# The recurrent mixer in another order: keys and queries of all heads first, values later, gates and u beside inverses and scans, levels and inverses in batches

## The chip, the cores and the metric

The kernel runs on one core of one Trainium2 chip. The number that counts is the device time of one execution in microseconds (us). Before the change it is 1601.41 us, the median of 3 runs (1600.74 to 1604.13). Engines are named as in the profile: PE is the matrix engine (PEld its weight loads), DVE the vector engine, ACT the scalar engine, POOL the general engine, SP the engine that issues the DMAs.

## What is computed

The reference is a block of two layers followed by a second block with sparse, dilated and cross attention. The change lies in the first mixer, which is run on 256 context tokens and 256 latent tokens together (512 columns here). It projects the normed input, and feeds two branches, a gated chunk mixer and a gated delta rule:

```
a_u, a_v, qkv, gate, alpha_raw, beta_raw = split(h @ w_in)
y_a = gelu(a_u) * (ws @ layer_norm(gelu(a_v)) + bs)      # chunks of 128 tokens, 4 groups
q, k, v = silu(dwconv3(qkv));  q, k = l2(q), l2(k)       # 4 heads of 128
T = inverse(I + strict_tril(beta k k^T * decay))         # per head, direction and chunk
S_t = a_t S_{t-1} (I - b_t k_t k_t^T) + b_t k_t v_t^T    # scan over chunks, forward and backward
o = rms_norm(o_forward + o_backward) * silu(gate)
y = concat(y_a, o) @ w_out
```

Everything is fp32 to the eye of the caller. A product of two matrices is made of three matmuls on rounded halves (hi and lo of the weight, hi and lo of the data), so one 1024 x 128 weight tile against 512 columns is 8 x 3 = 24 matmuls.

## The kernel before, in words

A tile framework schedules the program: the code is written stage by stage, pools give each tile name a number of buffers, and the framework lays all instructions out into one fixed order for each engine. An engine runs its list in order, so an instruction that waits holds back all that stands behind it. Parts under `high_priority` are put as early as their inputs allow. The pools of PSUM (the accumulators that PE writes) limit how many results can be in flight: `mm` for the wide products, `s1`, `lv`, `su` for the small ones of the recurrent branch.

Layer 0 before the change, with the time at which it runs in the trace:

- `gmlp` (to 51 us the a_v product, then to 74 us the a_u product, then the chunk mix with `wsT`, an elementwise product, 16 transposes and copies into `ya`).
- `gdn`: `stage1(h)` for heads 0 to 3. Each projects K, Q and V of one head (3 x 24 matmuls of 512 columns), evacuates with the three-tap convolution (line 751, DVE), transposes, makes the norms, the decay matrix `AT` and the strict triangle, which goes through memory to `blocks` (16 x 16 inverses by elimination, on DVE, 30 instructions for each direction on 64 partitions) and to `levels` (merging 16 to 32 to 64 to 128 by 32 x 32 and 64 x 64 matmuls). Parts of the modulation product (`ps_ad<-rawa`) are put between them by the list `GF`.
- `inverses(0)`, the four gate projections, then with new pools `inverses(2)` beside `scan(0)` (240 to 299 us). A scan carries four chains (two heads, two directions) through four steps; one step is up to five 128 x 128 matmuls into one `su` tile, with r (DVE, line 1255), vn (ACT, line 1258), the state S (DVE, line 1267) and o (line 1277 or ACT) between them. Three `su` tiles exist.
- `out("w_out0a", ...)` over the gmlp half (96 matmuls of 512 columns) beside `scan(1)`, then `out("w_out0b", ...)` twice: context columns beside the end of `scan(1)`, latent columns after it. Then the norm of the FFN and its first matmul, `ps_mm<-fh`, at 377 us.

In before the helper `mm` is line 366, the weight halves are made by ACT `whi` (line 344) and DVE `wlo` (line 345), a transpose is line 389. The DMA of a weight chunk is line 350, that of the modulation weights (`rawa`) line 640. In the changed file these lines are one lower.

Of the kernel before, what the change touches and what calls it, by code (L numbers as in the profile page):

```python
# [10 lines left out]
F32 = mybir.dt.float32  # L11
# [15 lines left out]
SWAP = ()  # L27
# [3 lines left out]
ROOT = ('pre', 'gmlp', 'gdn', 'ffn0', 'mla', 'ffn1', 'sparse')  # L31
# [10 lines left out]
GF = (6, 6, 4, 0, 0, 8)  # L42
SPS = (3, 3)
FILL = (12, 4)
AUN = 2
# [110 lines left out]
def _layout(x):  # L156
# [24 lines left out]
    vec["abs"] = x["a_bs"][0].T  # L181
# [21 lines left out]
    o["w_au"] = _tm(w[:, 0:512], 2)  # L203
# [4 lines left out]
    w = _fm(x["ab_w_out"][0]).reshape(4, 2, P, 2, 512).transpose(3, 0, 2, 1, 4).reshape(2, 4, P, 1024)  # L208
    o["w_out0a"], o["w_out0b"] = w[0], w[1]
# [53 lines left out]
class K:  # L263
# [127 lines left out]
    def rsqrt(self, v, n, scale=1.0, eps=EPS, plus=None):  # L391
# [4 lines left out]
        T = lambda dt=F32: self.small.tile([P, 16], dt, name=self.nm("rq"), tag="rq", bufs=12)[:, :n]  # L396
# [511 lines left out]
    def layer0(self):  # L908
        nc, d = self.nc, self.d
# [6 lines left out]
        yap = self.pool("ya")  # L916
        yp = yap.__enter__()
        ya = [yp.tile([P, 512], F32, name=f"ya{g}", tag=f"ya{g}", bufs=1) for g in range(4)]
        self.psum(mm=4, sm=2, ad=2)
        with self.pool("ring0") as self.ring, self.pool("aring0") as self.aring:  # L920
            self.RAW, self.HL, self.RAWA = 2, 2, 16
            gmp = self.pool("gm")
            gm = self.gmlp(gmp.__enter__(), hi, lo, ya)
# [19 lines left out]
            next(gm, 0)  # L943
            gmp.__exit__(None, None, None)
        self.phase("gdn")
        self.fillers = [f for j in range(4, 10) for f in self.ada4(0, j)]
        g1p = self.pool("gdn")
        g1 = g1p.__enter__()
        self.psum(mm=2, s1=3, lv=2, ad=1)
        g3p = self.pool("gdn3")  # L950
        g3 = g3p.__enter__()
        with self.pool("ring1") as self.ring, self.pool("gdn2") as g2:
            self.RAW, self.HL = 2, 2
            self.aring, self.RAWA = g2, 4
            inverses, scan = self.gdn(g1, g2, g3, hi, lo)
        hpool.__exit__(None, None, None)
        xp = self.ctx.enter_context(self.pool("xp", side="right"))
        self.x = xp.tile([P, 8, 512], F32, name="x", tag="x", bufs=1)
        ypool = self.pool("y0", side="right")
        yp2 = ypool.__enter__()  # L960
        self.outer(nr=1, ad=1, su=SPS[1])
        self.psum(lv=SPS[0])
        spool = self.pool("scan", side="right")
        scan = scan(spool.__enter__(), lambda h, s, o: self.split(o, yhi[:, 4 + h, s], ylo[:, 4 + h, s]))
        yhi = yp2.tile([P, 8, 512], F32R, name="yhi", tag="yhi", bufs=1)
        ylo = yp2.tile([P, 8, 512], F32R, name="ylo", tag="ylo", bufs=1)
        for k in range(4):
            self.split(ya[k], yhi[:, k], ylo[:, k])
        inverses(2)
        g3p.__exit__(None, None, None)  # L970
        with self.tc.high_priority():
            scan(0)
        for k in range(8):
            nc.sync.dma_start(self.x[:, k], d["x0"][:, k])
        self.psum(mm=SPS[0])

        def out(w, k0, a, b, tag="mm"):

            for j in range(4):
                wh, wl = [w.rearrange("p (i k m) -> p i k m", i=2, k=4) for w in self.chunk(d[w][j])]  # L980
                for i in range(2):
                    ps = self.ps(tag)
                    for k in range(4):
                        self.mm3(ps[:, :b - a], (wh[:, i, k], wl[:, i, k]), (yhi[:, k0 + k, a:b], ylo[:, k0 + k, a:b]),
                                 k == 0, k == 3)
                    for h, (u, v) in enumerate(halves):
                        if a <= u and v <= b:
                            xj = self.x[:, 2 * j + i, u:v]
                            nc.vector.scalar_tensor_tensor(xj, ps[:, u - a:v - a], m[:, 16 + 2 * j + i, 1 - h:2 - h], xj,
                                                           op0=ALU.mult, op1=ALU.add)  # L990
        yring = self.pool("yring")
        self.ring, self.RAW, self.HL = yring.__enter__(), 2, 3
# [16 lines left out]
    def gmlp(self, gp, hi, lo, ya):

        nc, d = self.nc, self.d
        lng = gp.tile([P, 512], F32, name="lng", tag="lng", bufs=1)
        lnb = gp.tile([P, 512], F32, name="lnb", tag="lnb", bufs=1)
        ws = gp.tile([P, 4, P], F32, name="wsT", tag="wsT", bufs=1)
        v = gp.tile([P, 4, 512], F32, name="gv", tag="gv", bufs=1)
        u = gp.tile([P, 4, 512], F32, name="gu", tag="gu", bufs=1)
        st = gp.tile([P, 4, 6], F32, name="gst", tag="gst", bufs=1)
        mv = gp.tile([P, 4, 2], F32, name="gmv", tag="gmv", bufs=1)
# [6 lines left out]
        for _ in range(4):  # L1025
# [27 lines left out]

    def gdn(self, g1, g2, g3, hi, lo):
# [13 lines left out]
        pt = self.ps("lv")  # L1068
# [20 lines left out]
        for di in range(2):  # L1089
            pc = self.ps("lv")  # L1090
# [5 lines left out]
        rq2 = T("rq2", 1, (P, 4, 4))  # L1096
# [842 lines left out]
```

## Time and profile before

| what | value |
|---|---|
| median of 3 runs | 1601.41 us |
| the profiled execution | 1601.92 us, of which the span from first to last instruction is 1600.1 us |
| mean granted PE clock | 0.974 |
| busy over the span | PE 1543.2 us (96%), DVE 1137.7 (71%), ACT 778.1 (49%), POOL 203.8 (13%) |
| DMA | 246.74 MB, 154 GB/s on average |

The profiled execution is 0.5 us above the median of the runs. PE is nearly always busy over the whole program, so time can be won only in the stretches where it isn't, or where its granted clock is below 1.0. The slices of the page show two such places, both in layer 0: in the slices of 40 us from 200 us on the granted clock reads 8, 5 and 8 tenths, where nearly all others read 9; and near 370 us, at the end of layer 0, PE waits again. The rows below go there.

### The profile page before, as it was taken

To read this page: it belongs to the slowest core of one execution; us is meant where nothing else is said; L and a number is where in the kernel's file an instruction comes from. 1 tells how busy PE (TensorE), PEld (TensorE's weight loads), DVE (VectorE), ACT (ScalarE), POOL (GpSimd) and SP (SyncE) were. 2 spreads that over 40 slices of the span, in tenths; PEclk is the share of its full clock that TensorE was granted. 3 is DMA by queue.
4 is the path that set the end of the run, shared out by engine and by line. 5 is a ranking of instruction groups with operands and counts; after the bars stand their busy time and mean duration, and the time that the engine had idled before them with its cause. 6 is when DMAs were issued, how large, how long until landed. Compare 5 with 4: busy or idle time off the path is not lost.

```text
span 1600.1 us, 27482 instructions
## 1 busy us (share of the span) xinstructions
PE 1543.2 (96%) x10518; PEld 1325.5 (83%) x10518; DVE 1137.7 (71%) x2418; ACT 778.1 (49%) x1418; POOL 203.8 (13%) x191
## 2 busy tenths in 40 slices
PE   7999889999999999999999999999999999999997
PEld 4767667888888888888777799998898898889996
DVE  4556854567999895875677688988798666655655
ACT  4377733445432342354555555656445555454443
POOL 0412100100120110110000011212332010001111
PEclk9999985899999999999999999999999999999998
DMA  8356532324556674634122356564545245346553
GB/s 343 115 201 188 167 84 78 101 106 151 170 184 217 217 237 147 203 115 150 39 63 91 122 169 191 175 196 151 183 137 168 70 134 184 109 145 192 188 183 105
DMA packets 97268, 246.74 MB, mean 154 GB/s; under 512 B 25328, under 2 KB 38512, under 8 KB 96624
## 3 DMA queue, kind: packets, MB, share of 16 engines
q1 hardware_dynamic: 96848, 244.45, 47.4%
q8 instruction: 83, 1.36, 0.3%
q10 hardware_dynamic: 288, 0.52, 0.1%
q14 instruction: 49, 0.40, 0.1%
HBM read 236.82 MB, written 8.13 MB: 153 GB/s over the span
## 4 chain that ended last, share of the span: by engine, by line
PE 87%; DVE 5%; DMA 4%; ACT 3%; issue 1%; SPq 1%; ACTq 0%; DVEq 0%
PE ps_mm L366 51%; PE ps_dn L366 17%; PE ps_nr L366 4%; PE ps_s L366 4%; PE ps_su L366 3%; PE ps_po L366 2%; PE ps_lv L366 1%; DVE wlo L345 1%; DMA rawa<-in_ada 1%; PE ps_pt L389 1%; ACT whi L344 1%; PE ps_ad L366 1%; DMA kvl<-kvd 1%; PE ps_kv L366 1%; DMA raw<-in_w_qkvg 1%
## 5 line engine op out<-in xcount | busy, mean ns | idle before, releaser
L344 ACT ACTIVATE whi<-raw 128x1024 fp32r<-128x1024 f32 (+2 forms) x345 | 345.2, 1008 | 416.6 <-PE ps_mm L366 214.7
L345 DVE TENSOR_TENSOR wlo<-raw,whi 128x1024 fp32r<-128x1024 f32 (+2 forms) x334 | 397.2, 1195 | 148.3 <-ACT whi L344 146.3
L366 PE MATMUL ps_mm<-fh,whi 128*128 128x258 f32 (+2 forms) x728 | 241.4, 333 | 2.5 <-ACT fh L513 1.5
L366 PE MATMUL ps_mm<-fh,wlo 128*128 128x258 f32 (+2 forms) x728 | 240.9, 332 | 0.0
L366 PE MATMUL ps_mm<-fl,whi 128*128 128x258 f32 (+2 forms) x728 | 240.8, 331 | 0.0
L366 PEld LDWEIGHTS ps_mm<-fh,whi 128*128 128x128 f32 x728 | 137.8, 190 | 15.6 <-ACT fh L513 1.8
L366 PEld LDWEIGHTS ps_mm<-fh,wlo 128*128 128x128 f32 x728 | 137.4, 189 | 13.3 <-issue 0.4
L366 PEld LDWEIGHTS ps_mm<-fl,whi 128*128 128x128 f32 x728 | 137.9, 190 | 12.7
L813 POOL TENSOR_TENSOR act<-cg,cu 128x512 f32<-128x512 f32 (+1 forms) x44 | 76.3, 1734 | 464.3 <-DVE cu L751 313.9
L366 PE MATMUL ps_dn<-ah,whi 128*128 128x256 f32 (+1 forms) x366 | 115.9, 319 | 1.6 <-ACT whi L344 1.2
L366 PE MATMUL ps_dn<-ah,wlo 128*128 128x256 f32 (+1 forms) x366 | 115.6, 318 | 0.1
L366 PE MATMUL ps_dn<-al,whi 128*128 128x256 f32 (+1 forms) x366 | 115.2, 316 | 0.0
L676 DVE CUSTOM_DVE_ANT_0 junk<-rawa,cb,vec 128x1024 f32<-128x1024 f32 x80 | 112.5, 1406 | 0.6
L366 PEld LDWEIGHTS ps_dn<-ah,whi 128*128 128x128 f32 x366 | 68.5, 188 | 8.9 <-ACT whi L344 2.4
L366 PEld LDWEIGHTS ps_dn<-ah,wlo 128*128 128x128 f32 x366 | 68.7, 188 | 6.1 <-DVE wlo L345 0.5
L366 PEld LDWEIGHTS ps_dn<-al,whi 128*128 128x128 f32 x366 | 68.7, 188 | 4.6
L366 PE MATMUL ps_mm<-hml,whi 128*128 128x256 f32 x256 | 72.5, 283 | 0.0
L366 PE MATMUL ps_mm<-hmh,wlo 128*128 128x256 f32 x256 | 72.4, 283 | 0.0
L366 PE MATMUL ps_mm<-hmh,whi 128*128 128x256 f32 x256 | 72.3, 283 | 0.0
L366 PE MATMUL ps_mm<-hh,whi 128*128 128x256 f32 (+1 forms) x224 | 65.7, 295 | 2.1 <-DVE z L1717 1.7
L366 PE MATMUL ps_mm<-hl,whi 128*128 128x256 f32 (+1 forms) x224 | 64.2, 288 | 0.0
L366 PE MATMUL ps_mm<-hh,wlo 128*128 128x256 f32 (+1 forms) x224 | 63.8, 286 | 0.0
(648 smaller groups left out, 3865.5 us busy)
## 6 DMA issues: line engine op xcount, KB each, us to landing
raw<-in_up SPq DMA_DIRECT2D x88, 512.0 KB, 3.6
rawa<-in_adt SPq DMA_DIRECT2D x56, 512.0 KB, 4.3
rawa<-in_ada SPq DMA_DIRECT2D x40, 512.0 KB, 7.8
raw<-in_dn SPq DMA_DIRECT2D x40, 448.0 KB, 3.3
raw<-in_w_u SPq DMA_DIRECT2D x32, 512.0 KB, 3.5
raw<-in_w_d SPq DMA_DIRECT2D x32, 512.0 KB, 4.3
raw<-in_w_qkvg SPq DMA_DIRECT2D x16, 512.0 KB, 3.9
raw<-in_dn SPq DMA_DIRECT2D x16, 512.0 KB, 3.5
```

Of the source, the lines that this page charges most:

```text
L344: self.nc.scalar.activation(hi, src, AF.Copy)
L345: (eng or self.nc.vector).tensor_tensor(lo, src, hi.bitcast(F32), op=ALU.subtract)
L366: self.nc.tensor.matmul(out, lhsT, rhs, start=start, stop=stop, **kw)
L389: self.nc.tensor.transpose(out, in_, self.ident[:in_.shape[0], :in_.shape[0]])
L676: self.nc.vector.tensor_tensor_reduce(o, r, self.cb[:, c], 1.0, self.v(f"ada_b{l}", i), ALU.mult, ALU.add, m[:, i, c:c + 1])
L813: nc.gpsimd.tensor_tensor(a, cg, cu, op=ALU.mult)
```

## The change

In words:

- `gmlp` keeps only the a_v product and the layer norm. The a_u product is made after the gates, in feature-major form, and the chunk mix is 16 matmuls of 128 x 128 that give feature-major results at once. The 16 transposes and the copies go. The bias is a tile of 256 KB loaded by DMA.
- `stage1(h)` projects only K and Q. `values(h)` projects V of the four heads afterwards. `blocks(0)`, `inverses(0)` and `blocks(2)`, `inverses(2)` and `scan(0)` are emitted under high priority.
- `blocks` treats both directions in one pass on 128 partitions (30 instructions for two heads instead of 60). `levels` treats two heads in one instruction and writes into `AT`.
- PSUM: `su` has two tiles, which levels and scans share (before: three `su` tiles for the scans and other ones for the levels).
- `w_out0a` covers the gmlp half and heads 0 and 1 (6 of 8 row blocks, 144 matmuls of 512 columns), `w_out0b` only heads 2 and 3 (48 matmuls of 256 columns for each half of the columns).
- One ring of weight buffers for the whole layer, three instead of four buffers for the modulation weights, `GF` (6, 6, 6, 6) instead of (6, 6, 4, 0, 0, 8).
- `SWAP` and `ROOT`: in this mixer and the sparse attention the three matmuls of a product are issued in another order, and some reciprocal roots take another order of products. Counts stay.

```diff
-SWAP = ()
+SWAP = ('gdn', 'sparse')
...
-GF = (6, 6, 4, 0, 0, 8)
-SPS = (3, 3)
+GF = (6, 6, 6, 6)
...
-        self.psum(mm=2, s1=3, lv=2, ad=1)
...
+        self.outer(ad=1, su=2)
+        self.psum(mm=2, s1=3)
+        self.aring, self.RAWA = g2, 3
+        stage1, values, chain, inverses, scan, proj = self.gdn(g1, g2, g3, sp, hi, lo)
+        first = self.tc.high_priority
+        stage1(0)
+        self.fill(GF[0])
+        chain()
+        stage1(1)
+        self.fill(GF[1])
+        with first():
+            chain(0)
+        stage1(2)
+        self.fill(GF[2])
+        stage1(3)
+        self.fill(GF[3])
+        with first():
+            inverses(0)
+            chain(2)
+        for h in range(4):
+            values(h)
+        with first():
+            inverses(2)
+            scan(0)
...
+        for h in range(4):
+            proj(12 + h, gate[h])
+        self.gemm([d["w_au"][g] for g in range(4)], 8, P, hi, lo, 512,
+                  lambda g, ps: nc.scalar.activation(u[g], ps, AF.Gelu))
...
+        for g in range(4):
+            mix(g, u[g])
+            ready(g, u[g], everything)
+        for h in range(2):
+            o = scan.outs[h]
+            nc.gpsimd.tensor_tensor(o, o, gate[h], op=ALU.mult)
+            ready(4 + h, o, everything)
         with self.tc.high_priority():
-            scan(0)
...
-        self.outer(nr=1, ad=1, su=SPS[1])
-        self.psum(lv=SPS[0])
...
-        inverses(2)
...
-        out("w_out0a", 0, 0, 512)
-        with self.tc.high_priority():
-            scan(1)
+            scan(1, gate, lambda h, s: ready(4 + h, scan.outs[h], s))
...
+        for j in range(8):
+            wh, wl = [w.rearrange("p (k m) -> p k m", k=6) for w in self.chunk(d["w_out0a"][j])]
+            ps = self.ps("mm")
+            for k in range(6):
+                self.mm3(ps, (wh[:, k], wl[:, k]), (yhi[:, k], ylo[k]), k == 0, k == 5)
+            add(ps, j, both)
...
+        last(0, "mm")
         self.outer(nr=1, ad=1)
         self.psum(mm=4, dn=2)
...
+        last(1, "mm")
...
-        au = self.gemm_tm_steps([d["w_au"][c] for c in range(4)], 8, 2, hi, lo, 4,
-                                lambda t, ps: nc.scalar.activation(u[:, t], ps, AF.Gelu))
...
+        nc.sync.dma_start(bs.rearrange("p g i -> p (g i)"), d["abs"][0].partition_broadcast(P))
...
-            self.mm(p3, ws[:, g], v[:, :, sl], True, True)
...
+                self.mm(ps[:, t * P:(t + 1) * P], v[:, t, g * P:(g + 1) * P], ws[:, g], True, True)
...
         def stage1(h):
-            kr, q, vr = T2("w", 4), T2("w", 4), T2("w", 4)
+            kr, q = T2("w", 4), T2("w", 4)
             proj(4 + h, kr)
             proj(h, q)
-            proj(8 + h, vr)
...
+        def values(h):
+            vr, vt = T2("w", 4), T("vt", 4)
+            proj(8 + h, vr)
+            act(vt, trs(vr), AF.Copy)
...
-        weave(one(0), one(1))
...
+        for n in range(15):
+            j = 15 - n
+            pr = T("pr")[:, :j, :n + 1]
+            nc.vector.tensor_tensor(pr, bl[:, :j, j:j + 1].to_broadcast([P, j, n + 1]),
+                                    iv[:, j:j + 1, j:].to_broadcast([P, j, n + 1]), op=ALU.mult)
+            nc.vector.tensor_tensor(iv[:, :j, j:], iv[:, :j, j:], pr, op=ALU.subtract)
```

Three places show how the instructions move.

The first is PE where `scan(0)` begins. In before the matmuls of the scan (`ps_su`) stand among those of the levels of heads 2 and 3 (`ps_lv`):

```order
L366 MATMUL ps_su_3150<-S_644_3107,kf_941 128x128
L366 MATMUL ps_lv_2803<-dc_2799,AT_1970 32x32 x7
L366 MATMUL ps_su_3167<-S_649_3120,kf_941 128x128
L366 MATMUL ps_lv_2803<-dc_2799,AT_1970 32x32 x5
L366 MATMUL ps_su_3137<-vn_657_3141,kdc_658_3143 128x128
L366 MATMUL ps_lv_2803<-dc_2799,AT_1970 32x32 x2
L366 MATMUL ps_lv_2821<-tc_2723,xc_2725 32x32 x5
L366 MATMUL ps_su_3150<-r_662_3154,DT_2112 128x128
```

In after the same scan has no levels beside it: the first steps stand among the last u tile, the chunk mix and two tiles of `w_out0a`, and from here on its matmuls stand alone, on two `su` tiles in turn:

```order
L365 MATMUL ps_su_520_2596<-vn_523_2603,kdc_524_2605 128x128
L365 MATMUL ps_su_514_2579<-qg_170_796,S_498_2536 128x128
L365 MATMUL ps_su_514_2579<-aT_515_2580,vn_517_2586 128x128
L365 MATMUL ps_su_520_2596<-qg_176_814,S_503_2549 128x128
L365 MATMUL ps_su_520_2596<-aT_521_2597,vn_523_2603 128x128
L365 MATMUL ps_su_526_2613<-S_508_2562,kf_206_978 128x128
L365 MATMUL ps_ad_538_2647<-ones_65,osq_539_2648 128x1
L365 MATMUL ps_su_532_2630<-S_513_2575,kf_206_978 128x128
L365 MATMUL ps_su_526_2613<-r_528_2617,AT_169_795 128x128
```

The wide products that stood beside the scan's end have moved behind it, and the levels have moved ahead of the scan, among gates and u.

The second is DVE where V of head 1 is evacuated in after. `pr` and `iv` are the elimination of `blocks(0)`, `AT` and `aT` belong to head 2, `w_447` is V of head 1, and its PSUM tile `ps_mm_452` is one of two:

```order
L1325 TENSOR_TENSOR pr_273_1199<-bl_256_1150,iv_258_1152 128x15
L1200 TENSOR_TENSOR aT_322_1381<-ps_s1_321_1372,AT_310_1339 128x512
L1200 TENSOR_TENSOR aT_323_1389<-ps_s1_321_1372,AT_316_1357 128x512
L1327 TENSOR_TENSOR iv_258_1152<-iv_258_1152,pr_273_1199 128x15
L1187 TENSOR_TENSOR kd_318_1365<-ps_s1_315_1355,gc_124_645 128x4
L1190 COPY ge_319_1368<-qg_317_1358 128x4
L1203 SCALAR_TENSOR_TENSOR AT_310_1339<-ps_s1_320_1371,beta_123_643,AT_310_1339 128x128 x4
L1203 SCALAR_TENSOR_TENSOR AT_316_1357<-ps_s1_320_1371,beta_123_643,AT_316_1357 128x128 x2
L1328 COPY br_257_1151<-iv_258_1152 64x256
L1203 SCALAR_TENSOR_TENSOR AT_316_1357<-ps_s1_320_1371,beta_123_643,AT_316_1357 128x128 x2
L344 TENSOR_TENSOR wlo_618_2856<-raw_616_2853,whi_617_2855 128x1024
L750 SCALAR_TENSOR_TENSOR w_447_2094<-ps_mm_452_2102,vec_63,w_447_2094 128x2x255
```

In before the same place holds the evacuations between single elimination steps, for example:

```order
L751 SCALAR_TENSOR_TENSOR w_1511<-ps_mm_1588,vec,w_1511 128x2x255
L1152 SCALAR_TENSOR_TENSOR AT_1684<-ps_lv_1682,gc_814,c_757 128x128
L1303 TENSOR_TENSOR pr_1415<-bl_1407,iv_1409 64x15
L399 TENSOR_SCALAR rq_1634<-ss_1625 128x4
L1303 TENSOR_TENSOR pr_1417<-bl_1411,iv_1413 64x15
L751 SCALAR_TENSOR_TENSOR w_1511<-ps_mm_1588,vec,w_1511 128x2x255
L1306 TENSOR_TENSOR iv_1409<-iv_1409,pr_1415 64x15
```

The elimination as a whole has moved ahead of the evacuation of V.

The third is SP's list of loads near the end of the a_v product. Before:

```order
L1035 DMA wsT<-in_wsT 128x512
L350 DMA raw_406<-in_w_av 128x1024
L350 DMA raw_494<-in_w_av 128x1024
L350 DMA raw_541<-in_w_au 128x1024
L350 DMA raw_571<-in_w_au 128x1024
```

After:

```order
L1066 DMA wsT<-in_wsT 128x512
L1067 DMA gbs<-in_abs 128x512
L639 DMA rawa_854<-in_ada 128x1024
L639 DMA rawa_860<-in_ada 128x1024
L639 DMA rawa_866<-in_ada 128x1024
L349 DMA raw_402<-in_w_av 128x1024
L349 DMA raw_490<-in_w_av 128x1024
```

Four loads, 256 KB and three of 512 KB, have moved ahead of the last two chunks of the a_v weight.

## Rows read from the trace of the kernel before

**Rows 1.** the page's chain that ended last, shares of the span by engine

```profile
PE 87%; DVE 5%; DMA 4%; ACT 3%; issue 1%; SPq 1%; ACTq 0%; DVEq 0%
```

**Rows 2.** windows: stretch, length, busy us (instructions) per engine, clock, DMA

```profile
51.00:81.00 30.00, 29.47 (x144) 21.98 (x147) 16.20 (x30) 10.83 (x17) 16.96 (x18) 1.00 0.20 68
81.00:180.00 99.00, 98.67 (x563) 73.94 (x556) 66.77 (x206) 72.66 (x136) 18.44 (x14) 1.00 0.57 188
180.00:240.00 60.00, 49.28 (x679) 37.32 (x678) 34.23 (x141) 30.44 (x75) 6.06 (x14) 0.86 0.43 114
240.00:247.00 7.00, 5.56 (x113) 4.25 (x111) 5.63 (x20) 4.49 (x15) 0.00 (x0) 1.00 0.74 229
247.00:288.00 41.00, 41.00 (x437) 32.49 (x438) 16.25 (x59) 13.81 (x45) 3.83 (x11) 0.50 0.13 37
350.00:356.00 6.00, 4.48 (x34) 3.41 (x34) 4.26 (x15) 2.41 (x6) 0.00 (x0) 1.00 0.75 273
356.00:377.00 21.00, 17.83 (x130) 14.21 (x129) 14.45 (x37) 12.06 (x23) 0.00 (x0) 0.91 0.81 295
```

**Rows 3.** windows, two stretches between 180 and 240 us

```profile
192.00:203.00 11.00, 7.69 (x74) 6.82 (x78) 3.85 (x10) 8.49 (x18) 1.26 (x1) 0.53 0.13 50
216.00:223.00 7.00, 4.70 (x13) 3.68 (x14) 6.13 (x33) 2.99 (x8) 0.00 (x0) 0.53 0.00 1
```

**Rows 4.** timeline of PE: start, length, instruction [idle, releaser]

```profile
194.65 1.12 PE L389 MATMUL ps_s<-c,kt 128*128 128x128 f32 x4 [4.45 <-DVE kt L1137]
...
218.30 0.31 PE L366 MATMUL ps_s<-tc,xc 32*32 32x32 f32 x2 [2.37 <-ACT xc L1358]
```

**Rows 5.** windows, the loads of the a_v stage

```profile
10.00:30.00 20.00, 18.45 (x148) 10.87 (x150) 10.78 (x35) 8.22 (x17) 0.00 (x0) 1.00 1.03 410
```

**Rows 6.** timeline of PE: a_v, matmuls of 512 columns, levels

```profile
40.67 0.50 PE L366 MATMUL ps_mm<-wlo,h0hi 128*128 128x512 f32 x1 [0.24 <-DVE wlo L345]
...
179.92 0.39 PE L366 MATMUL ps_mm<-h0hi,wlo 128*128 128x512 f32 x1
180.14 0.39 PE L366 MATMUL ps_mm<-h0hi,whi 128*128 128x512 f32 x1
...
184.80 0.45 PE L366 MATMUL ps_lv<-dc,AT 32*32 32x32 f32 x32
185.19 0.50 PE L366 MATMUL ps_mm<-h0lo,whi 128*128 128x512 f32 x1
...
236.00 0.96 PE L366 MATMUL ps_s<-DT,X 64*64 64x64 f32 x16
236.89 1.93 PE L366 MATMUL ps_ad<-rawa,sc 128*32 128x256 f32 x32
```

**Rows 7.** timeline, one scan step: matmul and what reads it, three places

```profile
288.50 0.49 PE L366 MATMUL ps_su<-S,kf 128*128 128x128 f32 x2
...
289.03 0.35 DVE L1255 SCALAR_TENSOR_TENSOR r<-ps_su,neg,vt 128x128 f32<-128x128 f32 x1 [1.02 <-PE ps_su L366]
...
316.08 0.39 PE L366 MATMUL ps_su<-r,DT 128*128 128x128 f32 x2
...
316.51 0.37 ACT L1258 ACTIVATE vn<-ps_su,beta 128x128 f32<-128x128 f32 x1 [2.05 <-PE ps_su L366]
...
345.72 0.39 PE L366 MATMUL ps_su<-aT,vn 128*128 128x128 f32 x2
...
346.21 0.29 DVE L1277 TENSOR_TENSOR o<-ps_su,o 128x128 f32<-128x128 f32 x1 [0.39 <-PE ps_su L366]
```

**Rows 8.** timeline, the last norm and the layer's end

```profile
349.90 0.16 DVE L1210 SCALAR_TENSOR_TENSOR ms<-ps_nr,rq 128x4 f32<-128x4 f32 x1
...
354.55 0.71 ACT L344 ACTIVATE yhi<-o 128x256 fp32r<-128x256 f32 x2
...
369.77 0.38 PE L366 MATMUL ps_mm<-yhi,wlo 128*128 128x256 f32 x1
...
377.00 1.01 PE L366 MATMUL ps_mm<-fh,whi 128*128 128x256 f32 x3 [1.53 <-ACT fh L513]
```

More of the change, by code (lines that the diff above doesn't have):

```diff
@@ L958, in layer0 @@
         self.x = xp.tile([P, 8, 512], F32, name="x", tag="x", bufs=1)
+        for k in range(8):
+            nc.sync.dma_start(self.x[:, k], d["x0"][:, k])
         ypool = self.pool("y0", side="right")
         yp2 = ypool.__enter__()
-        self.outer(nr=1, ad=1, su=SPS[1])
-        self.psum(lv=SPS[0])
-        spool = self.pool("scan", side="right")
-        scan = scan(spool.__enter__(), lambda h, s, o: self.split(o, yhi[:, 4 + h, s], ylo[:, 4 + h, s]))
         yhi = yp2.tile([P, 8, 512], F32R, name="yhi", tag="yhi", bufs=1)
-        ylo = yp2.tile([P, 8, 512], F32R, name="ylo", tag="ylo", bufs=1)
@@ L967, in layer0 @@
-        for k in range(4):
-            self.split(ya[k], yhi[:, k], ylo[:, k])
-        inverses(2)
-        g3p.__exit__(None, None, None)
-        with self.tc.high_priority():
-            scan(0)
[L973 to L990, printed above, removed]
@@ new lines, in layer0, with last @@
+        self.phase("wout0")
+        both = tuple(enumerate(halves))
+        for j in range(8):
[4 more added lines that the diff above has]
+            add(ps, j, both)
+        ws = [[w.rearrange("p (i k m) -> p i k m", i=4, k=2) for w in self.chunk(d["w_out0b"][c])] for c in range(2)]
+        def last(h, tag):
+            a, b = halves[h]
+            for j in range(8):
+                wh, wl = ws[j // 4]
+                ps = self.ps(tag)
+                for k in range(2):
+                    self.mm3(ps[:, :256], (wh[:, j % 4, k], wl[:, j % 4, k]), (yhi[:, 6 + k, a:b], ylo[6 + k][:, a:b]),
+                             k == 0, k == 1)
+                add(ps, j, both[h:h + 1], a)
@@ L1185, in gdn @@
[L1185 to L1207 removed]
+        def values(h):
+            vr, vt = T2("w", 4), T("vt", 4)
+            proj(8 + h, vr)
+            act(vt, trs(vr), AF.Copy)
+            H[h, 0]["vt"] = H[h, 1]["vt"] = vt
@@ new lines, in inverses, with chain @@
+        def inverses(h):
+            weave(*[self.levels(T3, c1, di, H[h, di]) for di in range(2)])
+        def chain(h=None):
+            if h is None:
+                zt = T2("ug", 1)
+                nc.vector.memset(zt, 0.0)
+                for c in (0, 4):
+                    nc.sync.dma_start(self.dz[c:c + 4].rearrange("c t p n -> p (c t) n"), zt.rearrange("p (a n) -> p a n", n=32))
+            else:
+                self.blocks(T3, c1, H, h)
+        U = lambda tag, bufs, shape=(P, 512): self.t(sp, shape, tag, bufs)
@@ new lines, in scan, with half @@
+        def scan(p, gate=None, done=None):
+            outs, first, late = scan.outs, set(), []
+            def half(i):
+                pb = self.ps("ad")
+                for h, t in late:
+                    o = outs[h][:, tl[t]]
+                    sq = U("osq", 2, (P, P))
+                    act(sq, o, AF.Square)
+                    c = 2 * (t - 2 * i) + h - 2 * p
+                    self.mm(pb[:, c:c + 1], sq, self.ones[:, 0:1], True, True)
+                    if gate:
+                        nc.gpsimd.tensor_tensor(o, o, gate[h][:, tl[t]], op=ALU.mult)
@@ L1278, in one @@
                     late.append((h, t))
-            return pair
-        return inverses, scan
+            for step in range(4):
+                for h in (2 * p, 2 * p + 1):
+                    for di in range(2):
+                        one(step, h, di)
+                if step % 2:
+                    half(step // 2)
+        scan.outs = [U("o", 4) for _ in range(4)]
+        return stage1, values, chain, inverses, scan, proj
     @staticmethod
@@ L1333, in levels @@
         yield 1
-        pz = p4()
-        for t in range(4):
+        pz = ps(32)
+        for t in N:
             for r in R:
@@ L1353, in levels @@
             nc.gpsimd.tensor_copy(D[r, :, o:o + 32], d2[r])
-        px = p4()
-        for t in range(4):
+        px = ps(32)
+        for t in N:
             for a, b in ab:
@@ L1360, in levels @@
         yield 1
-        pz = p4()
-        for t in range(4):
+        pz = ps(32)
+        for t in N:
             for a, b in ab:
```

270 lines of the change are left out of this document (108 added, 162 removed).

## The prediction

> **What bounds the kernel now.** I read the chain of waits first: 87% of it is PE [rows 1], so the program goes as fast as PE is fed, and a change counts where PE waits or runs at the lower clock. Then I cut layer 0 into windows [rows 2]. From 81 to 180 us PE is busy 98.67 of 99 us at clock 1.00: nothing to win there. From 180 to 240 it is busy 49.28 of 60, clock 0.86. From 240 to 247, where scan(0) begins, 5.56 of 7. From 247 to 288, scan(0) beside the levels of heads 2 and 3, PE is busy all 41 us at clock 0.50, the 1.2 GHz level: full, but at half speed. From 350 to 356 it is busy 4.48 of 6, from 356 to 377 17.83 of 21 at 0.91. So layer 0 loses 10.7 + 1.4 + 1.5 + 3.2 us by waiting, and about 20 us by the low clock from 247 to 288. Two smaller stretches at 0.53 [rows 3] hold 7.69 and 4.70 busy us, and at full clock they would take 0.53 of that: another 5.8 us lost. The timeline says what went before: PE stood 4.45 us for DVE's kt, and 2.37 us for ACT's xc [rows 4]. Some 43 us is the most that a better order could bring.
>
> **The change part by part.** I replace the stretch of before from 51 us (end of a_v) to 377.0 us (first `ps_mm<-fh` [rows 8]), 326 us, by a sum for the new order; what follows has the same instructions and I take it as 0, with 3 us to either side for the other order of products in the sparse phase.
>
> *A, late loads.* Four loads, 1.83 MB, now stand ahead of the last two a_v chunks on SP. The queues are full there: 410 GB/s from 10 to 30 us [rows 5], so 4.5 us later. The wait for the second-last chunk already showed on PE, 0.24 us [rows 6], so nothing covers it: +4.5 (bounds 0 and 5).
>
> *B, from the a and b projection to the last u tile.* Before: 81 to 240 us, PE busy 98.67 + 49.28 = 147.9 us, less the 5.8 us of half clock: 142 us of work at full clock. It holds the 16 tiles of K, Q, V and gates, stage1, the modulation parts and the levels of heads 0 and 1. Added are the u product, 4 x 24 matmuls of 512 columns at 0.228 us (starts 0.22 and 0.23 apart [rows 6]), 21.9 us, and the levels of heads 2 and 3, 416 matmuls of 32 x 32 at 0.39/32 and 64 of 64 x 64 at 0.89/16 us [rows 6], 5.1 + 3.6, of which part overlaps; I take 6. Sum 170. What PE will wait in B isn't in the trace. Below it is 0; above it is the rate of before, (11.1 idle + 5.8 clock)/142 of 170, 20 us. I take 10, a bit over half: the elimination on DVE falls from 120 to 60 instructions, and the gates and u, 44 us of wide matmuls at the end of B, ask DVE only for weight halves and so cover the levels of heads 2 and 3. B = 180.
>
> *C, mix, the first tiles of `w_out0a`, scan(0).* Behind the last u tile stand 16 matmuls of 128 x 128 for the mix (0.22 each, half of the pair of records at 288.50 [rows 7] and of its length: 3.5), 24 of `w_out0a` (5.5), 6 of 16 chain steps (28 matmuls, 5.7 with their neighbours), and 2 for hand-overs: 16.7. The first order piece of the front shows that 10 chain steps are left and stand alone, two `su` tiles in turn, so five rounds. One step holds its tile for: matmul to r 0.53, r 0.35, matmul to vn 0.43, vn 0.37, matmul to o 0.49, o 0.29 [rows 7], 2.46, and four hand-overs back to PE, which I put at 0.17 each: 3.15. Five rounds 15.8. Then `w_out0a` needs heads 0 and 1, normed: from `ms` at 349.90 to the end of the split at 355.26 it took 5.4 us [rows 8], with squares and sums some 7, under which only the start of scan(1) lies. PE does 2.0 us in 3.15 here, less than in the 5.56 of 7 us after which the clock fell at 247 [rows 2], so I add 4 us for a spell at 1.2 GHz. C = 16.7 + 15.8 + 7 + 4 = 43.5.
>
> *D, `w_out0a` beside scan(1).* 120 matmuls of 512 columns, 27.4; some 45 scan matmuls at 0.22, 9.9; the context half of `w_out0b`, 48 of 256 columns at half of 0.228, 5.5; 1 for waits: 43.8. Before had 96 + 192 such pieces; the two products are the same sum.
>
> *E, the end of scan(1).* The last 13 scan matmuls stand behind the context half and have no cover: 1.75 rounds, 5.5, and the norm, 6.3 with squares: 11.8. Before, the same end lay beside the first half of `w_out0b` and cost 1.5 us of waits [rows 2].
>
> *F, the latent half and the FFN norm.* 48 matmuls, 5.5; 3 for the clock, which E will have lowered as the window from 356 did (0.91 [rows 2]); then from the last product at 369.77 to the first `fh` at 377.00, 7.2 [rows 8], as before. F = 15.7.
>
> Sum: 4.5 + 180 + 43.5 + 43.8 + 11.8 + 15.7 = 299.3 us against 326: 26.7 us less. The profiled execution has 1601.92, the median of the runs 1601.41, 0.5 less, so 1574.7; I write 1575.
>
> The edits without a term: the chunk mix by 16 small matmuls drops 16 transposes and the stage from 74 to 81 us, which the sum has by leaving that stage out; `values` moves V's matmuls and issues the same 4 weight loads; the x loads and the 32 `aT` loads stand in SP's line with the weight chunks of `w_out0a`, and DMA moves 37 GB/s from 247 to 288 [rows 2], so there is room. `RAWA` 3 for 4 holds a modulation part back by one buffer, beside K and Q with the DMA at 188 GB/s of the 410 seen: 0.
>
> **A rule against it.** Before the clock fell at 247 us PE had been busy 5.56 of 7 us, with waits of at most a few tenths of a us between scan matmuls, and it stayed at 0.50 while busy all 41 us [rows 2]. The Trainium skill, "TensorE: Matmul & The Clock Gate", section "A second HAM failure mode: psum-queue depth-cycling", says that a kernel which takes a new PSUM tile in each round and idles a little between the groups goes back and forth between the two clocks. The trace agrees for scan(0) of before, and the bare rounds of C are more of that kind; by this rule the sum would be that of rival 2.
>
> **The rivals.**
>
> 1. *All covers hold.* No waits in B (-10), no low clock in C and F (-7), the late chunks hidden (-4.5): 1553. For it: 81 to 180 us shows that this mixture runs without a gap [rows 2]. Against: DVE was already busy 66.77 of 99 us there.
>
> 2. *The bare scan runs at 1.2 GHz to its end.* Each round has 2.0 us of matmuls, 10 us in five rounds and 2 in the norm, all of which doubles: +12 for the 4 taken: 1583; with the first tiles of D as well, 1587. For it: the 41 us at 0.50 [rows 2]; against: there the fill was 32 x 32 work, and here dense products stand on either side.
>
> 3. *What is won is lost again.* B waits at the rate of before (+10), rival 2 (+12), and E costs a few us more: 1599, no change. For it: E and the bare rounds are new waits on the path.
>
> 4. *DVE sets the pace of K, Q and V.* Place: the evacuations of V behind the elimination (the second order piece), with two `mm` tiles for PE to go on with. DVE was busy 101 of 159 us from 81 to 240 [rows 2], a share of 0.64. Gates and u, 44 us, stand at the end of B and ask little of it, so nearly all of the 101, less what the halved elimination saves, falls into the other 136 us: 0.74. Each time DVE is late PE stands as at 194.65, 4.45 us [rows 4], and the 7.69 us at 0.53 behind it cost 3.6 [rows 3]: 8 us. My 10 in B is 1.25 such waits. From 4.7 on, five of them, the gain is gone; six make 1613. There are up to eight places (four heads in stage1, four values), so it is possible; against it, before met just one of that size in its eight.
>
> That the change doesn't do what it says is in part in the sum: scan(0) was to run beside gates and u, but in the order its first matmul stands near the last u tile, since the levels of heads 2 and 3 hold the two `su` tiles till then.
>
> **How the numbers follow.** The forecast has 0.50, rival 1 0.13, rival 2 0.16, rival 3 0.10, rival 4 0.11. Its own range, from the bounds of A (-4.5, +0.5), B (10 to either side), C (-4, +8) and the rest (3 to either side), taken together by squares, is 1562 to 1589. For 8 in 10 it reaches to rival 1 below and rival 3 above: 1552 to 1603. About 0.2%, 3.2 us, is what a measurement of this kernel can tell: faster is below 1598.2, slower above 1604.6. Faster: 0.50 + 0.13 + 0.16, and a little of rival 3, 0.81; the same: most of rival 3, 0.07; slower: rival 4 and the tail of 3, 0.12.
>
> **What would show it.** A: a PE wait of 4 to 5 us for a_v's weight. B: the last u tile ends about 184 us after a_v. C: scan(0) alone for about 16 us, then a gap of some us at the norm, with the clock below 1.0 in part. D: some 44 us dense. E: a stretch of 12 us with PE half idle near 335 us. First `fh` at about 350 us, and the rest unchanged. It is wrong if `fh` comes after 374 us, if K, Q and V show waits for DVE of over 20 us, or if the part behind `fh` moves by more than 3 us.

## The result and the profile after

The changed kernel takes 1611.1 us (median of 4 runs, 1609.86 to 1612.81), the kernel before, run beside it, 1601.3 us (1600.74 to 1604.13). The ratio is 1.0058, 95% interval 1.0041 to 1.0076: slower by about 0.6%, where 1.7% faster was forecast. The profiled execution took 1610.69 us, with a span of 1608.9 us and a mean granted clock of 0.983; against that of before it is 8.8 us longer. First, the page: PE in part 1, and part 4, the chain that ended last:

```profile
PE 1532.9 (95%) x10478; PEld 1312.1 (82%) x10478; DVE 1133.9 (70%) x2333; ACT 763.7 (47%) x1374; POOL 189.8 (12%) x164
PE 80%; DVE 11%; ACT 3%; issue 3%; DMA 2%; SPq 0%; POOL 0%; ACTq 0%; DVEq 0%
```

PE is idle for 76.0 of the 1608.9 us, where it was idle for 56.9 of 1600.1: 19.1 us more. Beside [rows 1] the share of PE in the chain has gone from 87 to 80, that of DVE from 5 to 11 and that of issue (time for which the profile shows no releaser) from 1 to 3. The chain passes through other engines also where PE is busy, so these shares say where to look and not how long PE waits. The windows cut layer 0 at the borders of the forecast's terms A, B, C, D, E and F; the last row is the start of the FFN (columns as in [rows 2]).

```profile
51.20:56.90 5.70, 5.70 (x26) 4.50 (x25) 1.51 (x3) 3.24 (x5) 0.00 (x0) 1.00 0.29 92
56.90:255.80 198.90, 184.85 (x1840) 138.53 (x1839) 120.14 (x318) 109.18 (x215) 34.58 (x34) 0.96 0.47 142
255.80:299.30 43.50, 39.06 (x252) 32.93 (x250) 26.73 (x83) 17.40 (x52) 2.17 (x2) 1.00 0.28 89
299.30:344.90 45.60, 45.08 (x261) 38.66 (x261) 28.41 (x70) 13.98 (x30) 2.18 (x5) 1.00 0.21 65
344.90:359.70 14.80, 8.22 (x55) 6.08 (x53) 5.07 (x22) 6.36 (x13) 1.83 (x4) 0.84 0.44 151
359.70:379.80 20.10, 16.38 (x91) 11.76 (x91) 10.16 (x31) 9.36 (x22) 0.00 (x0) 0.84 0.42 145
379.80:387.00 7.20, 6.35 (x33) 6.06 (x34) 6.83 (x19) 3.12 (x7) 0.00 (x0) 0.59 0.51 163
```

| term | forecast, us | measured, us |
|---|---|---|
| A, late loads | 4.5 | 5.8 |
| B, to the last u tile | 180 | 198.9 |
| C, mix and scan(0) | 43.5 | 43.5 |
| D, `w_out0a` beside scan(1) | 43.8 | 45.6 |
| E, end of scan(1) | 11.8 | 14.8 |
| F, latent half and norm | 15.7 | 20.1 |
| first `ps_mm<-fh`, against before | -26.7 | +2.8 |
| all that follows | 0 | +6.0 |

B holds most of it: PE is idle for 14.05 of its 198.9 us. The timeline of PE shows where, and the waits of A, E and F (start, length, instruction, in brackets the idle time before it and what ended it):

```profile
44.09 1.81 PE L365 MATMUL ps_mm<-whi,h0hi 128*128 128x512 f32 x4 [3.86 <-ACT whi L343]
...
154.57 1.50 PE L365 MATMUL ps_ad<-rawa,sc 128*32 128x256 f32 x24 [1.92 <-DVE adat L661]
156.39 0.63 PE L388 MATMUL ps_s<-c,w 128*128 128x128 f32 x4 [0.32 <-DVE kd L1187]
162.58 0.77 PE L365 MATMUL ps_mm<-h0hi,whi 128*128 128x512 f32 x1 [5.57 <-DVE w L750]
...
169.30 1.39 PE L365 MATMUL ps_su<-dc,AT 32*32 32x32 f32 x128
170.54 1.30 PE L365 MATMUL ps_su<-tc,xc 32*32 32x32 f32 x118
174.01 0.31 PE L365 MATMUL ps_su<-tc,xc 32*32 32x32 f32 x10 [2.17 <-issue]
...
220.48 0.58 PE L365 MATMUL ps_su<-tc,xc 32*32 32x32 f32 x26 [3.44 <-issue]
...
353.93 1.16 PE L365 MATMUL ps_ad<-c,rq 128*128 128x128 f32 x8 [2.04 <-DVE rq L409]
...
359.69 1.22 PE L365 MATMUL ps_mm<-yhi,whi 128*128 128x256 f32 x4 [2.39 <-ACT yhi L343]
...
379.78 1.01 PE L365 MATMUL ps_mm<-fh,whi 128*128 128x256 f32 x3 [3.72 <-ACT fh L512]
```

The 5.57 us wait ends with DVE's convolution `w`, which frees an `mm` tile. What DVE did before shows in its own timeline:

```profile
142.14 0.37 DVE L1321 COPY bl<-br 64x256 f32<-64x256 f32 x1 [2.27 <-DMA br<-atd]
142.55 0.99 DVE L1325 TENSOR_TENSOR pr<-bl,iv 128x15 f32<-128x15 f32 x1
...
158.04 0.37 DVE L1328 COPY br<-iv 64x256 f32<-64x256 f32 x1
158.45 0.61 DVE L1203 SCALAR_TENSOR_TENSOR AT<-ps_s,beta,AT 128x128 f32<-128x128 f32 x2
158.98 1.22 DVE L344 TENSOR_TENSOR wlo<-raw,whi 128x1024 fp32r<-128x1024 f32 x1
160.11 0.74 DVE L750 SCALAR_TENSOR_TENSOR w<-ps_mm,vec,w 128x510 f32<-128x510 f32 x1
```

The elimination (line 1325) begins when its copy gets the DMA `br<-atd`, for which DVE stood 2.27 us with all that is queued behind. Then elimination and the `AT` of another head alternate until 158.45. Only at 160.11 does DVE drain the first of the two `mm` tiles that PE has long filled. In the two other long waits of B the profile names issue: no semaphore that it shows held PE back, in the middle of a run of 32 x 32 matmuls. These runs are long here: 256 and 288 records without another matmul between them (two records for each matmul), where before's longest has 128.

The clock in windows: at the end of A, at three places of B, at 247 to 288 us, and at the start of F:

```profile
44.40:47.90 3.50, 3.50 (x10) 2.65 (x9) 2.23 (x3) 0.59 (x1) 0.30 (x1) 0.51 0.21 40
160.50:167.30 6.80, 4.72 (x11) 3.78 (x12) 4.91 (x16) 2.54 (x3) 0.00 (x0) 0.50 0.95 239
174.10:177.50 3.40, 3.40 (x20) 2.19 (x19) 0.80 (x2) 2.65 (x8) 0.80 (x2) 0.50 0.02 5
218.50:225.30 6.80, 4.82 (x75) 4.07 (x75) 1.23 (x3) 2.35 (x6) 0.83 (x3) 0.50 0.01 2
247.00:288.00 41.00, 38.34 (x244) 32.47 (x243) 22.42 (x63) 14.16 (x39) 0.00 (x0) 1.00 0.29 93
359.70:365.30 5.60, 5.60 (x23) 4.57 (x23) 1.65 (x4) 1.17 (x4) 0.00 (x0) 0.50 0.40 162
```

At 247 to 288 us, where before ran at 0.50, it is now 1.00. It fell to 0.50 at three places of B instead, all behind those waits. The 12.93 us that PE was busy there cost 6.5 us.

### The profile page after: what moved, and what is told of

The parts are those of the page before. It is cut to its first block, busy times and chain, and to the rows that moved or that the text cites. A ratio compares the mean times of both kernels' runs of the same rounds, so it can differ in the third digit from the quotient of the medians.

```text
span 1608.9 us, 27218 instructions
## 1 busy us (share of the span) xinstructions
PE 1532.9 (95%) x10478; PEld 1312.1 (82%) x10478; DVE 1133.9 (70%) x2333; ACT 763.7 (47%) x1374; POOL 189.8 (12%) x164
## 3 DMA queue, kind: packets, MB, share of 16 engines
q8 instruction: 82, 1.34, 0.3%
## 4 chain that ended last, share of the span: by engine, by line
PE 80%; DVE 11%; ACT 3%; issue 3%; DMA 2%; SPq 0%; POOL 0%; ACTq 0%; DVEq 0%
PE ps_mm L365 47%; PE ps_dn L365 16%; PE ps_nr L365 4%; PE ps_s L365 4%; DVE wlo L344 3%; PE ps_su L365 3%; PE ps_po L365 2%; DVE junk L675 1%; PE ps_ad L365 1%; PE ps_pt L388 1%; ACT whi L343 1%; PE ps_sm L365 1%; DVE cg L750 1%; DVE cu L750 0%; DMA kvl<-kvd 0%
## 5 line engine op out<-in xcount | busy, mean ns | idle before, releaser
L343 ACT ACTIVATE whi<-raw 128x1024 fp32r<-128x1024 f32 (+4 forms) x343 | 341.3, 1002 | 389.3 <-PE ps_mm L365 212.5
L344 DVE TENSOR_TENSOR wlo<-raw,whi 128x1024 fp32r<-128x1024 f32 (+4 forms) x333 | 395.7, 1194 | 146.6 <-ACT whi L343 144.3
L365 PE MATMUL ps_mm<-h0hi,whi 128*128 128x512 f32 (+1 forms) x168 | 68.5, 408 | 5.6 <-DVE w L750 5.6
L365 PE MATMUL ps_mm<-h0hi,wlo 128*128 128x512 f32 (+1 forms) x168 | 68.4, 407 | 0.0
L365 PE MATMUL ps_mm<-h0lo,whi 128*128 128x512 f32 (+1 forms) x168 | 68.1, 406 | 0.0
```

The costliest lines, as they stand in the source:

```text
L343: self.nc.scalar.activation(hi, src, AF.Copy)
L344: (eng or self.nc.vector).tensor_tensor(lo, src, hi.bitcast(F32), op=ALU.subtract)
L365: self.nc.tensor.matmul(out, lhsT, rhs, start=start, stop=stop, **kw)
```

## The experiments

The theory after this reading: B is long because V's evacuations stand behind the elimination, because long 32 x 32 runs starve PE of instructions, and because of the loads in A; E and F are long because two scan tiles leave the end of scan(1) without cover. A rival: the batching and reordering simply hold more PE work than counted, so that undoing single waits gives little back. Times are medians; ratios are to the kernel before on the same chip. The time to the first `fh` is 379.78 us in the changed kernel.

**V of heads 0 and 1 ahead of the first elimination.**

```diff
-        with first():
-            chain(0)
+        values(0)
+        values(1)
+        with first(), self.behind(self.last):
+            chain(0)
+        values(2)
+        values(3)
...
-        for h in range(4):
-            values(h)
```

> The changed kernel, but the elimination of heads 0 and 1 comes after the evacuation of V of heads 0 and 1 on DVE. Theory 1 (the elimination standing ahead of the V evacuations made PE wait 5.57 us at 162.58 and 1.92 and 0.32 us just before, and cost some 2 us of half clock behind them): these waits go, the first fh matmul comes 8 to 10 us earlier, time about 1602. Rival (DVE is simply too full in the whole K, Q, V part, so the wait only moves): first fh within 2 us of 379.8, time about 1610.

Measured: 1602.63 us, ratio 1.0009 (1.0000 to 1.0018); first `fh` at 370.37. The windows of B and C:

```profile
57.20:242.90 185.70, 180.02 (x1801) 133.21 (x1800) 115.57 (x316) 107.00 (x211) 34.57 (x34) 0.98 0.49 152
242.90:289.80 46.90, 43.76 (x290) 36.28 (x288) 27.78 (x86) 19.03 (x57) 1.99 (x2) 1.00 0.26 82
```

B is 13.2 us shorter, its idle time falls from 14.05 to 5.7 us (3.3 of them one wait for a load of modulation weights), and no wait of 1 us or more for DVE is left in it. C gives 3.4 back. So this order gains about 9 us. It also splits the levels into shorter runs (at most 192 records in a row, instead of 256 and 288), and the issue waits shrink from 5.6 us to 0.7; the run does not say how much each has of the 9.

**The late loads put behind the last a_v chunk.**

`self.cut` is the last weight DMA issued, `late` that of the last a_v chunk.

```diff
-        self.nc.sync.dma_start(w[:, :f], ap)
+        self.cut = self.nc.sync.dma_start(w[:, :f], ap)
...
+            late = self.cut
...
-        self.fill(GF[0])
+        with self.behind(late):
+            self.fill(GF[0])
...
-        nc.sync.dma_start(bs.rearrange("p g i -> p (g i)"), d["abs"][0].partition_broadcast(P))
+        with self.behind(self.cut):
+            nc.sync.dma_start(bs.rearrange("p g i -> p (g i)"), d["abs"][0].partition_broadcast(P))
```

> The changed kernel, but the last two a_v weight chunks are issued ahead of the bias tile and of the three modulation parts, as in the kernel before. Theory (the wait of 3.86 us at 44.09 us is the late load): that wait goes and everything behind comes 3.5 to 4.5 us earlier, time about 1606.5. Rival (the wait is the norm's chain through ACT's h0hi, which the load only happens to meet): still over 3 us of wait there, time 1610 to 1611.

Measured: 1603.5 us, ratio 1.0039 (1.0005 to 1.0074); a_v ends at 50.75 instead of 56.95 us, and the 3.86 us wait is gone. That is 6.2 us at A, so the loads are the cause of A, with the half clock behind the wait, which went too. By the first `fh` (371.05) the gain is 8.7: B is 196.0 us, 2.9 less, with the low clock of 218 us absent though the issue wait before it, 2.14 us, was still there. Why the clock held there is open. The V wait stayed:

```profile
157.22 0.76 PE L365 MATMUL ps_mm<-h0hi,whi 128*128 128x512 f32 x1 [5.56 <-DVE w L750]
```

**Three `su` tiles, one taken from `s1`.**

```diff
-        self.outer(ad=1, su=2)
-        self.psum(mm=2, s1=3)
+        self.outer(ad=1, su=3)
+        self.psum(mm=2, s1=2)
```

> The changed kernel with three PSUM tiles for scans and levels and two instead of three for stage1 (su=3, s1=2). Theory (two su tiles pace the bare scan from 268 to 299 us and leave scan(1)'s end bare from 345 to 360 us): the stretch from the mix to the rest of w_out0a shrinks by 5 to 8 us and the bare end by 4 to 6 us, less what stage1 loses with one tile fewer (0 to 5): time 1600 to 1605. Rival (the end is paced by the norm chain and the scan by DVE and ACT, not by the tiles): within 2 us of 1610.

Measured: 1611.19 us, ratio 1.0065 (1.0050 to 1.0080), no change against the changed kernel, and not the 1600 to 1605 that were expected. B grew by 6.6 (205.5), C shrank by 2.7 (40.8), and E, the bare end of scan(1), halved:

```profile
350.70:358.40 7.70, 3.37 (x18) 1.95 (x16) 2.98 (x13) 2.88 (x5) 0.46 (x1) 0.70 0.76 256
```

So the number of scan tiles does set E, and stage1 pays for a tile taken from it.

**The old order of the three matmuls in the sparse phase.**

```diff
-SWAP = ('gdn', 'sparse')
+SWAP = ('gdn',)
-ROOT = ('pre', 'gmlp', 'mla')
+ROOT = ('pre', 'gmlp', 'ffn0', 'mla', 'ffn1', 'sparse')
```

> The changed kernel with the old order of the three products in the sparse phase (SWAP only in the first mixer) and the old form of the roots outside it. Theory (the changed order costs 2.3 us between 1286 and 1326 us, three waits of 0.8 us for x): the part behind 1126 us is 2 to 3 us shorter, time about 1608. Rival (those waits come from elsewhere, the order is free): no difference over 0.5 us there.

Measured: 1610.81 us, ratio 1.0065 (1.0049 to 1.0082); first `fh` at 379.70. Behind the first `fh` its profile is 0.9 us shorter (1228.2 us for 1229.1), the median of the whole 0.3, where 2 to 3 were expected: this order is not the +6.

**Two more tiles for the scans alone**, from the PSUM that is free once stage1 has ended. The same line gives the wide products a third `mm` tile.

```diff
+        self.psum(mm=3, sx=2)
         with first():
             inverses(2)
             scan(0)
...
-                pu = self.ps("su")
+                self.nsu = getattr(self, "nsu", 0) + 1
+                pu = self.ps(("su", "sx")[self.nsu % 2])
```

> The changed kernel, but behind the values the two PSUM tiles that stage1 no longer needs go to the scans (a second pair, used in turn with su), so four chain steps can be in flight, and stage1 loses nothing. Theory (the terms D, E and F came out 9 us larger than forecast because scan(1) on two tiles runs out of time and leaves its last steps and its norm bare from 345 to 360 us): the stretch from the last context product to the first latent product falls from 14.7 us to under 4, the bare scan from 268 to 299 shrinks by some us, first fh 10 to 14 us earlier, time about 1598. Rival 1 (the end is paced by DVE and ACT between the matmuls): bare end still over 10 us, time 1607 to 1611. Rival 2 (what was seen with three su tiles, where stage1 had one fewer, was all there is): under 3 us.

Measured: 1591.71 us, ratio 0.9936 (0.9917 to 0.9955): faster than both. First `fh` at 366.10, 13.7 earlier. Its C, D and E:

```profile
258.40:301.60 43.20, 42.48 (x326) 39.67 (x325) 29.91 (x98) 20.31 (x62) 3.18 (x4) 1.00 0.33 102
301.60:342.10 40.50, 40.50 (x234) 35.24 (x233) 23.96 (x67) 15.71 (x32) 3.88 (x7) 1.00 0.39 128
342.10:344.50 2.40, 0.16 (x2) 0.00 (x0) 1.62 (x3) 1.36 (x3) 0.00 (x0) 1.00 0.17 65
```

E goes from 14.8 to 2.4 us and D from 45.6 to 40.5, without a gap: scan(1) now ends beside `w_out0a`. Scan(0) no longer shares its tiles with the levels and begins at 202.72 instead of 249.22 us. A, B (200.3) and F (21.6) are longer, by 1.2, 1.4 and 1.5 us; in B the clock is 0.91 instead of 0.96. This is the largest single gain found. No run has the scan tiles without the third `mm` tile, so the 13.7 us are not shown to be theirs alone. For them speak the run with three `su` tiles, which halved E with two `mm` tiles, and that `w_out0a` does as much ahead of the norm of scan(0) as in the changed kernel, 24 matmuls. (The profiled execution took 1596.28 us, 4.6 above the median; the 13.7 us are of that execution.)

**Runs of 32 x 32 matmuls of known length.** In the first FFN, at six places, 32, 64, 96, 128, 192 and 256 such matmuls on data that is there are added, with results that nobody reads.

```diff
+            if l == 0 and g == 1 and j < 6:
+                pb = self.ps("ad")
+                z = acts[0][0].bitcast(F32)
+                for q in range((32, 64, 96, 128, 192, 256)[j]):
+                    r = slice(32 * (q % 4), 32 * (q % 4) + 32)
+                    c = 32 * (q // 4 % 16)
+                    self.mm(pb[r, c:c + 32], z[r, c:c + 32], z[r, 0:32], True, True, (r.start, r.start))
```

> The changed kernel with work added: in the down product of the second group of layer 0's FFN, ahead of the first six output tiles, runs of 32, 64, 96, 128, 192 and 256 matmuls of 32 x 32 on a tile that is long ready, whose result nothing reads. Nothing in a run waits for another engine. Theory (in a long run PE outruns the supply of its own instructions: the waits of 2.17 us at 174.01 and 3.44 us at 220.48 us inside runs of 32 x 32 matmuls, marked issue): no wait inside the runs of 32 to 96, one of 2 to 3.5 us inside each run of 128 or more. Rival (a semaphore of the levels that the profile does not show): no wait over 0.3 us inside any run.

Measured: 1643.7 us in a single execution, with the added work in it. The timeline of PE has two records for each matmul:

```profile
604.57 0.75 PE L365 MATMUL ps_ad<-ah 32*32 32x32 f32 x64
...
610.23 1.29 PE L365 MATMUL ps_ad<-ah 32*32 32x32 f32 x128
...
616.43 1.82 PE L365 MATMUL ps_ad<-ah 32*32 32x32 f32 x192
...
623.17 1.50 PE L365 MATMUL ps_ad<-ah 32*32 32x32 f32 x155
626.60 1.60 PE L365 MATMUL ps_ad<-ah 32*32 32x32 f32 x101 [1.93 <-issue]
...
633.93 2.39 PE L365 MATMUL ps_ad<-ah 32*32 32x32 f32 x261
638.45 1.24 PE L365 MATMUL ps_ad<-ah 32*32 32x32 f32 x123 [2.14 <-issue]
...
646.57 2.22 PE L365 MATMUL ps_ad<-ah 32*32 32x32 f32 x240
650.77 1.29 PE L365 MATMUL ps_ad<-ah 32*32 32x32 f32 x128 [1.98 <-issue]
654.23 1.93 PE L365 MATMUL ps_ad<-ah 32*32 32x32 f32 x128 [2.17 <-issue]
657.68 0.44 PE L365 MATMUL ps_ad<-ah 32*32 32x32 f32 x16 [1.53 <-issue]
```

None up to 96 matmuls, one wait in 128 and in 192, three in 256; from the second on they come after each 128 records, 64 matmuls. With their weight loads these are 256 instructions. The profile shows neither data nor a semaphore that is waited for, and the distance between the waits is a fixed number of instructions: PE works faster than its instructions arrive. The two issue waits of B, 5.6 us together, stand after 246 and 221 records of such runs and are of this kind.

**The first, second and fourth edit together**, and then **these with the two scan tiles**; last, the scan tiles and the loads alone. No new edits.

> The edits of e1, e2 and e4 together: V ahead of the elimination, a_v loads first, old product order in the sparse phase. Theory (their places are apart, so 9, 4.4 and 1.9 us add up): about 1595 to 1597, faster than before by about 0.3%. Rival (the half clock spells and waits move and eat part): 1600 or more.

> The edits of e5 and e7 together. Theory: e7 less what e5 wins, about 1583 to 1586, faster than before by about 1%. Rival (without waits in K, Q and V the scan's share is already hidden): 1592 or more.

> The edits of e5 (four tiles for the scans) and e2 (a_v loads first) on the changed kernel; the elimination stays ahead of V. Theory (places apart, costs add): 4.4 us under e5, about 1587, with a wait of 4 to 6 us for the V evacuation still there. Rival (a change of the half clock spells eats it, as e2 gained 7.6 and not 4.4): anything from 1582 to 1592 without that wait moving.

| kernel | median, us | ratio to before | first `fh` | B |
|---|---|---|---|---|
| three undone | 1598.87 | 0.9976 (0.9962 to 0.9990) | 368.63 | 187.1 |
| the same and two scan tiles | 1587.03 | 0.9907 (0.9882 to 0.9932) | 355.95 | 202.9 |
| scan tiles and loads | 1588.69 | 0.9941 (0.9907 to 0.9975) | 358.33 | 196.9 |

Expected were 1595 to 1597, 1583 to 1586 and about 1587 us; the first two came out higher. The tiles and the loads nearly add up to the first `fh`: 13.7 and 8.7 us alone, 21.5 together. The first edit does not: with the fourth, which moves nothing ahead of `fh`, it adds 2.4 of its 9.4 beside the loads, and 2.4 beside tiles and loads. In the first kernel of the table C has grown from 43.5 to 50.0, and scan(0) begins at 245.91 us, 8 us behind the last u tile, where it began 6.5 us ahead of its end. In the second C is 36.3, but PE waits in B anew, 2.91 us for a level's `dc` at 177.15 and 4.11 us at 187.72. For this one the profile names an `iv` of the second elimination, the last that DVE had ended; the matmul itself reads a `dc`, which DVE made at 187.12, behind a copy of that elimination that waited for a DMA:

```profile
185.11 0.37 DVE L1328 COPY bl<-br 64x256 f32<-64x256 f32 x1 [6.38 <-DMA br<-atd]
```

Its interval overlaps that of the last.

One order more was run, all edits with V of head 0 alone ahead of the elimination; about 1583 us was expected. Its results are wrong, for a reason that is open, so it is no version of the kernel, but its trace can be read. It takes 1586.54 us, ratio 0.9914 (0.9889 to 0.9939), with the first `fh` at 358.38, as with tiles and loads alone. The waits for `dc` at 177 and 188 us are gone, and in their place PE waits 4.30 us for `w` and 1.85 and 2.33 us for issue. So V of both heads has to stand ahead of the elimination for its wait to go. Of the kernels with right results, the second of the table is the fastest.

## Why the prediction was wrong

Two of the prediction's own signs of being wrong came: `fh` stands at 379.78 us, after 374, and the part behind it moved by 6.0, more than 3. The third did not: the waits of B for DVE are 7.8 us, not over 20.

**A** was right in place, and 5.8 us for 4.5: the wait is 3.86, and the half clock behind it (3.5 us busy at 0.51), which had no term, 1.7.

**B** is the step that failed: "What PE will wait in B isn't in the trace ... I take 10, a bit over half". Waits and clock cost 14.05 + 6.5 = 20.5 us, the upper bound, the rate of before. The reason given for the lower value, a halved elimination on DVE, looked at how much DVE does and not at what stands behind it. The chain was put early because its inputs come early, and on an engine that keeps its order it holds two V evacuations through a DMA wait and 16 us of alternation. The issue waits, 5.6 us and the clock behind them, were in no term: batching the levels made the 32 x 32 runs long enough for them. The work itself was also too low, 178.4 us (198.9 - 20.5) for 170. The levels are the largest share. In before half of the first pair's levels stand on the tile `lv` and half on `s1`, which the profile shows as `ps_s`:

```profile
L366 PE MATMUL ps_lv<-dc,AT 32*32 32x32 f32 x96 | 2.1, 201 | 0.0
L366 PE MATMUL ps_s<-dc,AT 32*32 32x32 f32 x96 | 1.8, 194 | 2.3 <-DVE dc L1345 2.3
```

An estimate that counts each matmul from its start to the start of the next, at the granted clock, gives 8.8 us for that pair and 18.0 for both pairs after the change, so the added pair has some 9.2 where 6 was taken for an overlap that did not come. By the same count the modulation parts have 2.5 us more than before's in its stretch (17.0 for 14.5). These two make 5.7 of the 8.4; no run tests them apart.

**C** came out at 43.5, with an error on either side. The clock stayed at 1.00, so the 4 us for a spell were not needed, and rounds and norm took 29.8 us instead of 15.8 + 7 + 4 = 26.8. The half clock from 247 to 288 us, which the windows of before showed as a loss, did go.

**D** was 1.8 over. **E** was in place and 3.0 us too small. In it PE waits for `rq` and `yhi`, 2.04 and 2.39 us, and the second has another cause than the tiles. ACT:

```profile
356.04 1.28 ACT L877 ACT_TABLE_LOAD   x1 [4.59 <-DMA cb<-in_crow]
357.33 2.00 ACT L877 ACTIVATE cb<-cb 128x1024 f32<-128x1024 f32 x2
359.24 0.70 ACT L343 ACTIVATE yhi<-o 128x256 fp32r<-128x256 f32 x2
```

In before `cb` came behind `yhi` (354.55 us [rows 8]):

```profile
359.42 1.06 ACT L878 ACTIVATE cb<-cb 128x1024 f32<-128x1024 f32 x1 [0.94 <-DMA cb<-in_crow]
```

`cb` belongs to the FFN. In the changed kernel it stands ahead of `yhi` in ACT's list and waited for its DMA; with the load of a function table before it, it held `yhi` until 359.24 us, though `o` was ready at 356.09. That is 3.15 us, about what E is over; it is read from the trace, and no run has moved `cb`. That the end of scan(1) stands bare at all, the prediction had taken from the two `su` tiles, and the runs bear this out: 7.7 us with one tile more, 2.4 with two and the third `mm` tile.

**F** was 4.4 us too small. The half clock that E brings cost 2.8 us, near the 3 taken. But from the first latent product to the last it took 11.1 us for 5.5 + 3, since the norm's sums (`ps_nr` and `ps_dn<-sq,ones`) stand among the products, and from the last product to `fh` 9.0 for 7.2.

**The rest** was not 0 but +6.0. About 2 us is the start of the FFN, where the clock is 0.59 for 7.2 us; some 1.6 lies at a spell near 819 us with the clock at 0.90 where before had 1.00. The other order in the sparse phase measured 0.9 us in one profile and nothing in the medians. The remainder is open.

Of the rivals, the third, "what is won is lost again", described the outcome best: B at the rate of before and E dearer. But 12 of its 24 us were for the bare scan, which did not come; in their place stand the work of B (8.4 us), D and F (6.2) and the rest (6.0). The fourth had the right mechanism, evacuations of V behind the elimination, and came near the time for another reason: it happened once (5.57 us and the 1.92 before it, with some 2.4 for the clock), not five times. The second, the bare scan at 1.2 GHz, did not occur: PE was busy 39.06 of 43.5 us in C, and waited between the steps, and the clock read 1.00 throughout. Nor did the clock go back and forth in scan(0) of before: it fell once, at 247 us, and stayed at 0.50 until 288 [rows 2]. The rule of the Trainium skill cited for it ("TensorE: Matmul & The Clock Gate", "A second HAM failure mode: psum-queue depth-cycling") is not borne out by these rounds; the clock of the changed kernel's B fell behind single waits of 2 to 5.6 us.

## What to carry to other kernels

An instruction that is put early on an engine that keeps its order is dear if it waits for a DMA: look at which evacuations stand behind it, and how many tiles PE has until then, rather than at the engine's busy share. It happened twice here, on DVE in B and on ACT in E. Count the accumulator tiles that a chain of dependent steps has in flight at its end; here one more made the difference between 14.8 us bare and 7.7, two more (with a third `mm` tile) that between 14.8 and 2.4. Work that is put together into a long run of tiny matmuls can outrun the supply of instructions, so mix it with wide ones: in the first experiment, which did so in part, 5.6 us of issue waits became 0.7.

## What the runs showed of the hardware

In the runs of known length PE waited 1.5 to 2.2 us for instructions, first after some 78 to 130 matmuls of 32 x 32 in a row and then after each 64. The page of the changed kernel has 82 packets and 1.34 MB in an instruction queue, 16.3 KB for a packet. PE has 20956 matmuls and weight loads there: 64 bytes for each, if that queue is PE's, and 256 of them in a packet. The Trainium skill, "Runtime: NRT & Kernel Launch", section "Instruction fetch mechanics", has the same blocks of 16 KiB and 256 instructions, but calls the cost of crossing one mostly hidden, because instructions are issued more slowly than they are fetched. Outside such runs the trace agrees: all of the 5.6 us that PE of the changed kernel waits for issue is in the two runs of levels. In these it does not, and the measurement decides.
